# More score buffers, a third buffer for turned exponentials and two more PSUM banks in the last dilated attention pair

## Chip, cores and metric

The kernel runs on one core of a Trainium2 chip. The metric is device microseconds of one execution. The engines are TensorE (PE in the profile, its weight loads PEld), VectorE (DVE), ScalarE (ACT), GpSimd (POOL) and SyncE (SP), which only issues transfers. SBUF holds the tiles, PSUM the results of matmuls.

## What is computed

One step of a decoder layer, for a prompt of 1024 positions and eight single tokens ("samples") that read a cache. A combined projection of `x` (1024 channels) feeds eight dilated softmax heads of 64 channels and four gated DeltaNet heads of 128; their outputs, side by side, go through `w_out`, a LayerNorm, and a two-level mixture of 32 experts.

```python
p = x @ w_in
# dilated head, three branches (window, dilation) = (128,1), (512,4), (2048,16):
s = q @ k.T * Dh**-0.5 + bias;  pr = exp(s - max(s));  o = (pr @ v) / sum(pr)
oa = merge of the three branches, weighted by their softmax denominators
# DeltaNet heads give ob
h  = layer_norm(alpha * x + concat(oa, ob) @ w_out)
x' = layer_norm(alpha * h + hier_moe(h))
```

In the kernel the three branches are one softmax over all earlier positions: the merge is folded into the bias, which is a huge number where no branch reads a key.

## The kernel before

The work runs in this order: the DeltaNet heads with their projections; four pairs of dilated heads (0 to 3); the product with `w_out` and the LayerNorm in tiles of 128 positions (`mixed` and `finish`, lines 1136 and 1173), with the samples' attention in between; routing; the experts. Instructions are written in Python order, and a scheduler then sets the order on each engine; each engine works strictly in that order. A tile pool with n buffers lets the scheduler run a writer ahead of the readers of the n-1 tiles before.

**A pair** (`attention`, line 833) is eight row blocks `i` of 128 positions, two heads `j` each. For one (i, j), with w = 128 (i+1) columns: scores in pieces of at most 512 columns, two matmuls each (L857, L858), into PSUM tiles `s` of the pool `pss` (two banks); DVE adds the bias, writes them to the score buffer `sc` and takes the row minimum `mx` (L859); ACT takes the exponential in place (L864); PE turns `sc` in 128x128 blocks into PSUM tiles `pps` (L873, two banks); ACT (L875) or DVE (L877) copies them into `pT`; PE multiplies `pT` with the values into `o` (L882). After four row blocks the sums are inverted (L884, L885), turned (`rps`, L888), and the half's result `moa` is formed by ACT (L890) and DVE (L891) and stored (L892). `sc` uses the two buffers of the slot `ktl`, `pT` the two of `vh`.

While pairs 0 to 2 run, the projections of the next pair fill PE's waits (`next(fill, None)`). Pair 3 has no next pair. What stands beside it instead is: the loads of `w_out` on ACT's queue (L1059), the split of its rows into a rounded part on ACT (L1061) and the rest on DVE (L1062, the first of eight on POOL); the samples' products with cached keys on POOL (L911), summed on DVE (L912); and what the scheduler can bring forward of tile 0 of the product with `w_out`. For tile t this is two halves of 512 columns, 24 matmuls each (L1142), into `op`, in the pool `mm` of two PSUM banks that the projections used; their operands are `mh` (slot `qk`, buffer t%2; shown as `qkm`) and `ml` (slot `zt`, buffer (t+1)%2; shown as `ztm`), made from `mt` by ACT (L1167) and DVE (L1168). In the program's names `wst` and `wr` are loaded rows of `w_out`, `wo` their split, `kc` cached keys, `qb` the samples' queries, `g` and `b` the LayerNorm's factors (slot `U`, buffers 0 and 1, loaded on POOL's queue at L1120 and L1121).

```python
minima.setdefault(pr, []).append(ii)
...
if k not in WOP:
    after(los[-k - 1], minima[p_][n])
after(his[-k - 1], exps[p_][max(n - 1, 0)])
```

These lines (from the end of the driver) tie each subtraction and rounding of `w_out` behind a certain row minimum or exponential of the pair, by the table `WOD`; the cached keys' sums are tied in the same way.

## Time and profile before

| what | value |
|---|---|
| runs | 1508.02 us median of 3 (1506.76 to 1508.31) |
| profiled execution | 1508.93 us, its span 1507.2 us |
| busy share of the span | PE 94%, PEld 77%, DVE 72%, ACT 58%, POOL 21% |
| last dilated pair | 668.9 to 733.0 us |
| tiles 0 and 1 of the product with `w_out` | matmuls end 750.3 us |
| half clock in the pair | 678.7 to 709.5 us |

The span runs from the first to the last instruction. In a timeline row the first number is the start in us of the span, the second the length of the row (several instructions of one kind in succession make one row, xcount), and brackets give the idle time of the engine ahead of it with what ended it. A matmul's length includes its way through the array, so two in succession overlap; the distance of two starts is what one costs. PEclk is TensorE's granted clock, 1.00 being 2.4 GHz and 0.50 being 1.2 GHz. One matmul of L882 stands in the trace as up to two records, so the counts of `o` in the timeline are larger than in the program.

### The profile page before, as it was taken

How to read it: one execution, taken by the hardware profiler on the slowest of the kernel's cores; microseconds unless marked ns; L12 is line 12 of the kernel's file. 1: busy time of each engine (PE TensorE's matmuls, PEld its weight loads, DVE VectorE, ACT ScalarE, POOL GpSimd, SP SyncE). 2: the span in 40 equal slices, each digit the busy share in tenths (PEclk: the TensorE clock that was granted, in tenths of full speed). 3: DMA queues.
4: the chain of work that ended last, by engine and by line, in shares of the span. 5: the costliest groups of instructions: out<-in, count | busy, mean ns of one | idle time of the engine just before them, and what ended most of it. 6: DMA issues, size and time to landing. Idle time of an engine off the chain costs nothing. (4 is left out here: it accounts for less than half of the span.)

```text
span 1507.2 us, 22545 instructions
## 1 busy us (share of the span) xinstructions
PE 1410.2 (94%) x7916; PEld 1165.7 (77%) x7917; DVE 1084.3 (72%) x2080; ACT 878.8 (58%) x1747; POOL 319.5 (21%) x322
## 2 busy tenths in 40 slices
PE   6989999998999999999999969999999999999990
PEld 5879888887987878775777758888888888888870
DVE  3676776756444536356545669999999999999986
ACT  4323534333243434345221149999999999999984
POOL 1030403224032240112301121111111222111113
PEclk9999999999999999995999969999999999999995
DMA  5321101102332344054972569999999999999966
GB/s 197 115 77 36 59 28 42 36 10 76 92 115 95 108 138 120 32 158 143 265 251 88 209 236 352 356 368 375 353 360 348 356 372 362 365 360 368 345 212 230
DMA packets 115262, 309.36 MB, mean 205 GB/s; under 512 B 13635, under 2 KB 43255, under 8 KB 115136
## 3 DMA queue, kind: packets, MB, share of 16 engines
q1 hardware_dynamic: 89848, 261.74, 47.1%
q0 software_dynamic: 14640, 33.51, 8.9%
q10 hardware_dynamic: 10656, 12.62, 2.7%
q8 instruction: 64, 1.05, 0.3%
q14 instruction: 54, 0.44, 0.1%
HBM read 284.04 MB, written 45.24 MB: 218 GB/s over the span
## 5 line engine op out<-in xcount | busy, mean ns | idle before, releaser
L1362 DVE TENSOR_TENSOR wl<-p,wh 128x512 fp32r<-128x512 f32 x436 | 270.3, 686 | 1.7 <-ACT wh L1361 1.7
L1361 ACT CAST wh<-p 128x512 fp32r<-128x512 f32 x436 | 254.1, 633 | 19.3 <-PE h L1398 9.0
L278 PE MATMUL pp<-xh,w 128*128 128x344 f32 x672 | 231.8, 345 | 15.3 <-ACT xh L315 11.8
L280 PE MATMUL pp<-xh,w 128*128 128x344 f32 x672 | 223.1, 332 | 1.3 <-DVE w L253 1.3
L279 PE MATMUL pp<-xl,w 128*128 128x344 f32 x672 | 222.9, 332 | 0.6 <-DVE xl L316 0.6
L1396 PE MATMUL h<-wh,eh 128*128 128x512 f32 x512 | 207.1, 404 | 0.0
L1397 PE MATMUL h<-wl,eh 128*128 128x512 f32 x512 | 205.9, 402 | 0.4 <-DVE wl L1362 0.4
L1398 PE MATMUL h<-wh,el 128*128 128x512 f32 x512 | 201.2, 393 | 0.0
L278 PEld LDWEIGHTS pp<-xh,w 128*128 128x128 f32 x672 | 130.2, 194 | 26.9 <-ACT xh L315 11.5
L280 PEld LDWEIGHTS pp<-xh,w 128*128 128x128 f32 x672 | 129.9, 193 | 4.2 <-issue 1.9
L279 PEld LDWEIGHTS pp<-xl,w 128*128 128x128 f32 x672 | 130.2, 194 | 1.9 <-DVE xl L316 1.0
L1397 PEld LDWEIGHTS h<-wl,eh 128*128 128x128 f32 x512 | 96.8, 189 | 25.4 <-DVE wl L1362 7.9
L1362 DVE TENSOR_TENSOR wl_d<-p,wh_d 128x512 fp32r<-128x512 f32 x188 | 115.6, 687 | 0.0
L1368 POOL MEMSET xg<- 128x1024 f32 x32 | 30.5, 953 | 398.8 <-PE xp L1381 397.3
L1396 PEld LDWEIGHTS h<-wh,eh 128*128 128x128 f32 x512 | 96.9, 189 | 18.8 <-ACT eh L1383 0.2
L1361 ACT CAST wh_d<-p 128x512 fp32r<-128x512 f32 x188 | 109.4, 621 | 3.2
L1398 PEld LDWEIGHTS h<-wh,el 128*128 128x128 f32 x512 | 96.6, 189 | 18.8 <-DVE el L1384 0.2
L1437 PE MATMUL py<-wh_d,al 128*128 128x512 f32 x248 | 96.9, 391 | 0.0
L1435 PE MATMUL py<-wh_d,ah 128*128 128x512 f32 x248 | 96.6, 389 | 0.0
L1436 PE MATMUL py<-wl_d,ah 128*128 128x512 f32 x248 | 96.5, 389 | 0.0
L864 ACT ACTIVATE sc<-sc,mx 128x128 f32<-128x128 f32 (+7 forms) x64 | 49.7, 776 | 78.1 <-DVE mx L859 71.4
L1142 PE MATMUL op<-wo,qkm 128*128 128x512 f32 x256 | 84.8, 406 | 0.0
(457 smaller groups left out, 2764.5 us busy)
## 6 DMA issues: line engine op xcount, KB each, us to landing
p<-in_w_up SPq DMA_DIRECT2D x58, 1024.0 KB
p<-in_w_gate SPq DMA_DIRECT2D x51, 1024.0 KB
p<-in_w_down SPq DMA_DIRECT2D x47, 1024.0 KB
rw<-in_w_cols SPq DMA_DIRECT2D x28, 512.0 KB
p_vh<-in_w_down SPq DMA_DIRECT2D x12, 512.0 KB
p_ktl<-in_w_gate SPq DMA_DIRECT2D x10, 512.0 KB
p_ktl<-in_w_down SPq DMA_DIRECT2D x10, 512.0 KB
skew_d<-bias_d SPq DMA_DIRECT2D x1, 4608.0 KB
```

The source lines that it names most:

```text
L278: nc.tensor.matmul(ps, wh[:, k, :], xh[:, k, s], start=(k == 0), stop=False)
L279: nc.tensor.matmul(ps, wh[:, k, :], xl[:, k, s], start=False, stop=False)
L280: last[c0, g] = nc.tensor.matmul(ps, wl[:, k, :], xh[:, k, s], start=False, stop=(k == KD - 1))
L1142: mixes[t] = nc.tensor.matmul(pss[b], m[:, k, :], wo[k][:, w, cs[b]], start=(k + i == 0), stop=(k + i == KD + 1))
L1361: nc.scalar.copy(out=wh, in_=src)
L1362: nc.vector.tensor_tensor(out=wl, in0=src, in1=wh.bitcast(F32), op=OP.subtract)
L1396: nc.tensor.matmul(ps, eh[:, k, :], wh, start=(k == 0), stop=False)
L1397: nc.tensor.matmul(ps, eh[:, k, :], wl, start=False, stop=False)
L1398: nc.tensor.matmul(ps, el[:, k, :], wh, start=False, stop=(k == KD - 1))
L1435: nc.tensor.matmul(py[b], ah[:, k, :], wh, start=(k == 0), stop=False)
L1436: nc.tensor.matmul(py[b], ah[:, k, :], wl, start=False, stop=False)
L1437: nc.tensor.matmul(py[b], al[:, k, :], wh, start=False, stop=(k == 3))
```

## The change

Only pair 3 is touched (`pr == 3`). With u = 2i + j:

- **Scores:** odd row blocks put `sc` into buffer 0 of slot `U` (head 0) or of slot `qk` (head 1) instead of `ktl`: four buffers in turn instead of two.
- **Turned exponentials:** every third `pT` goes to buffer 1 of slot `zt`: three in turn instead of two.
- **PSUM:** for row blocks 0 to 5, the pieces with even u + n_ go to a bank of the pool `mm`, so half of the scores use the projections' two banks.

The three borrowed buffers have users behind the pair: `U` 0 is the LayerNorm's `g` (L1120), `qk` 0 is tile 0's `mh`, `zt` 1 is tile 0's `ml`. The two banks are those of tile 0's `op`. In the changed file, the lines behind 853 are shifted by up to 4: L857 to L861, L859 to L863, L864 to L868, L873 to L877, L882 to L886, L888 to L892, L1142 to L1146, L1168 to L1172.

```diff
--- before.py
+++ after.py
@@ -848,11 +848,15 @@
                 pTs = []
                 for j in range(2):
                     pt = slice(64 * j, 64 * j + 64)
-                    sc = T4("ktl", f"sc{pr}_{i}_{j}")
+                    u = 2 * i + j
+                    sc = T4("ktl", f"sc{pr}_{i}_{j}") if pr < 3 or u % 4 < 2 else T4_at(("U", "qk")[j], 0, f"sc{pr}_{i}_{j}")
                     mx = sm2.tile([P, 2], F32, tag="mx", name=f"mx{pr}_{i}_{j}", bufs=4)
                     cuts = (0, w) if w <= 512 else (0, 384 if w == 640 else 512, w)
                     for n_, (c, e) in enumerate(zip(cuts, cuts[1:])):
-                        sps = pss.tile([P, 512], F32, tag="s", name=f"s{pr}_{i}_{j}_{c}")
+                        if pr < 3 or i > 5 or (u + n_) % 2:
+                            sps = pss.tile([P, 512], F32, tag="s", name=f"s{pr}_{i}_{j}_{c}")
+                        else:
+                            sps = mm.tile([P, 512], F32, tag="mm", name=f"s{pr}_{i}_{j}_{c}")
                         qi = slice(i * P, (i + 1) * P)
                         nc.tensor.matmul(sps[:, :e - c], qs[j][:, qi], ks[j][:, c:e], start=True, stop=False)
                         nc.tensor.matmul(sps[:, :e - c], qs[j][pt, qi], kl[pt, c:e], start=False, stop=True)
@@ -864,7 +868,7 @@
                     ex = nc.scalar.activation(out=sc[:, :w], in_=sc[:, :w], func=AF.Exp, scale=-1.0, bias=m, accum_out=lsum[:, i, j:j + 1])
                     exps.setdefault(pr, []).append(ex)
                     next(fill, None)
-                    pT = tiles(T4("vh", f"pT{pr}_{i}_{j}"))
+                    pT = tiles(T4("vh", f"pT{pr}_{i}_{j}") if pr < 3 or u % 3 < 2 else T4_at("zt", 1, f"pT{pr}_{i}_{j}"))
                     pTs.append(pT)
                     for c in range(0, i + 1, 4):
                         e = min(i + 1, c + 4)
```

The order of the instructions shifts with it. In the rows below, `s_2_0_0` is the score piece of row block 2, head 0, first column 0; `pps`, `sc` and `pT` are numbered by block and head; `o_0` and `o_1` are the pair's two halves; the last number is the buffer's own.

PE, near the opening of pair 3, before:

```order
L873 MATMUL pps_0_0_0_6157<-cm,sc_0_0_6149 128x128
L873 MATMUL pps_0_1_0_6168<-cm,sc_0_1_6160 128x128
L882 MATMUL o_0_6148<-pT_0_0_6156,vv_6049 64x128
L882 MATMUL o_0_6148<-pT_0_1_6167,vv_6049 64x128
L857 MATMUL s_2_0_0_6203<-ksa_6119,qs_6118 128x384
L858 MATMUL s_2_0_0_6203<-kl_6121,qs_6118 128x384
L857 MATMUL s_2_1_0_6216<-ksb_6120,qs_6118 128x384
L858 MATMUL s_2_1_0_6216<-kl_6121,qs_6118 128x384
L873 MATMUL pps_1_0_0_6181<-cm,sc_1_0_6173 128x128 x2
L873 MATMUL pps_1_1_0_6193<-cm,sc_1_1_6185 128x128 x2
L882 MATMUL o_0_6148<-pT_1_0_6180,vv_6049 64x128
L857 MATMUL s_3_0_0_6235<-ksa_6119,qs_6118 128x512
```

and in the changed kernel, from the scores of block 2 on:

```order
L861 MATMUL s_2_0_0_6203<-ksa_6119,qs_6118 128x384
L862 MATMUL s_2_0_0_6203<-kl_6121,qs_6118 128x384
L861 MATMUL s_2_1_0_6216<-ksb_6120,qs_6118 128x384
L877 MATMUL pps_0_0_0_6157<-cm,sc_0_0_6149 128x128
L862 MATMUL s_2_1_0_6216<-kl_6121,qs_6118 128x384
L886 MATMUL o_0_6148<-pT_0_0_6156,vv_6049 64x128
L861 MATMUL s_3_0_0_6235<-ksa_6119,qs_6118 128x512
L862 MATMUL s_3_0_0_6235<-kl_6121,qs_6118 128x512
L861 MATMUL s_3_1_0_6249<-ksb_6120,qs_6118 128x512
L862 MATMUL s_3_1_0_6249<-kl_6121,qs_6118 128x512
L877 MATMUL pps_0_1_0_6168<-cm,sc_0_1_6160 128x128
L861 MATMUL s_4_0_0_6282<-ksa_6119,qs_6118 128x384
```

The scores of blocks 2, 3 and the beginning of 4 now stand ahead of the turning of block 1; before, the turning of blocks 0 and 1 stood between them.

PE, the end of pair 3 and what stands behind it, before (`op_0_6582` and `op_1_6583` are the halves of tile 0):

```order
L1142 MATMUL op_0_6582<-wo_6105,qkm_6572 128x512
L873 MATMUL pps_7_1_0_6484<-cm,sc_7_1_6472 128x128 x4
L873 MATMUL pps_7_1_4_6490<-cm,sc_7_1_6472 128x128 x4
L1142 MATMUL op_0_6582<-wo_6105,qkm_6572 128x512
L1142 MATMUL op_0_6582<-wo_6105,ztm_6573 128x512
L1142 MATMUL op_0_6582<-wo_6110,qkm_6572 128x512 x2
L888 MATMUL rps_1_6514<-cm,rlb_6146 128x128 x4
L1142 MATMUL op_0_6582<-wo_6110,ztm_6573 128x512
L1142 MATMUL op_0_6582<-wo_6115,qkm_6572 128x512
L882 MATMUL o_1_6279<-pT_7_1_6483,vv_6049 64x128
```

and in the changed kernel, from the pair's last `o` on (`scps` are the samples' scores):

```order
L886 MATMUL o_1_6279<-pT_7_1_6483,vv_6049 64x128
L892 MATMUL rps_1_6514<-cm,rlb_6146 128x128 x4
L923 MATMUL scps<-cm,sc_388 64x128
L924 MATMUL scps<-cm,sc_389 64x97
L1146 MATMUL op_0_6582<-wo_6082,qkm_6572 128x512 x2
L1146 MATMUL op_1_6583<-wo_6082,qkm_6572 128x512 x2
L1146 MATMUL op_0_6582<-wo_6082,ztm_6573 128x512
L1146 MATMUL op_0_6582<-wo_6086,qkm_6572 128x512 x2
```

Before, 22 of the 24 matmuls of tile 0's first half stood between the last blocks of the pair; now all 48 of the tile stand behind the pair, and the first that needs `ztm` is the fifth.

DVE at the same place, before (`ztm_6573` is tile 0's, `ztm_6673` tile 1's; the other 896 columns of tile 0 stand six rows further up):

```order
L1168 TENSOR_TENSOR ztm_6573<-mt_6571,qkm_6572 128x128
L877 COPY pT_7_0_6459<-pps_7_0_0_6460 128x512
L859 ISA sc_7_1_6472,mx_7_1_6473<-s_7_1_512_6478,tb_6142,mx_7_1_6473 128x512
L859 ISA mx_7_1_6473 128x1
L884 RECIPROCAL lsum_6145<-lsum_6145 128x8
L885 COPY rlb_6146<-lsum_6145 128x512
L877 COPY pT_7_1_6483<-pps_7_1_4_6490 128x512
L891 TENSOR_TENSOR moa_6147<-moa_6147,o_1_6279 128x512
L1176 SCALAR_TENSOR_TENSOR h_6580<-h_6580,op_0_6582 128x512
L1168 TENSOR_TENSOR ztm_6673<-mt_6671,qkm_6672 128x1024
```

and in the changed kernel:

```order
L888 RECIPROCAL lsum_6145<-lsum_6145 128x8
L889 COPY rlb_6146<-lsum_6145 128x512
L881 COPY pT_7_1_6483<-pps_7_1_4_6490 128x512
L1172 TENSOR_TENSOR ztm_6673<-mt_6671,qkm_6672 128x1024
L895 TENSOR_TENSOR moa_6147<-moa_6147,o_1_6279 128x512
L1172 TENSOR_TENSOR ztm_6573<-mt_6571,qkm_6572 128x896
L1172 TENSOR_TENSOR ztm_6573<-mt_6571,qkm_6572 128x128
L927 ISA avs,mxs<-scps,dbias 64x225
L927 ISA mxs 64x1
```

Tile 0's `ztm` moved from ahead of the last turned exponentials to behind the pair's last `moa`, and tile 1's from behind `moa` to ahead of it.

On ACT, tile 0's roundings (L1167) moved from ahead of block 7's exponentials to behind the last copy of `pT_7_1`, and tile 1's stands between block 7's two exponentials in both. Near the opening, the exponential of block 0, head 0, now stands ahead of the sixth load of `w_out` (L1059) on ACT's queue, and that of block 1, head 0, ahead of the seventh. On POOL the load of `g` moved from ahead of the pair to behind the samples' first loads of cached values.

## Rows read from the trace of the kernel before

**Rows 1.** The profile's page, part 1: busy us, share of the span, instructions.
```profile
PE 1410.2 (94%) x7916; PEld 1165.7 (77%) x7917; DVE 1084.3 (72%) x2080; ACT 878.8 (58%) x1747; POOL 319.5 (21%) x322
```

**Rows 2.** Windows of the last pair and tile 0: us, busy time per engine, PEclk, DMA.
```profile
668.90:678.70 9.80, 8.27 (x41) 5.00 (x40) 4.73 (x15) 2.90 (x11) 2.27 (x4) 1.00 0.95 317
678.70:709.50 30.80, 28.25 (x105) 17.24 (x105) 20.09 (x37) 15.55 (x28) 8.94 (x3) 0.50 0.40 145
709.50:733.00 23.50, 23.50 (x172) 16.75 (x169) 14.28 (x31) 11.26 (x20) 9.20 (x14) 1.00 0.74 199
733.00:750.30 17.30, 17.30 (x76) 13.96 (x76) 9.52 (x12) 1.05 (x1) 2.87 (x5) 1.00 1.05 287
```

**Rows 3.** Timeline of PE, opening of the pair: start, us, instruction, idle before.
```profile
674.00 0.71 PE L873 MATMUL pps<-cm,sc 128*128 128x128 f32 x2 [0.34 <-ACT sc L864]
...
678.05 1.02 PE L873 MATMUL pps<-cm,sc 128*128 128x128 f32 x4 [1.07 <-ACT sc L864]
...
679.62 0.80 PE L857 MATMUL s<-ksa,qs 128*128 128x512 f32 x1
680.34 0.79 PE L858 MATMUL s<-kl,qs 64*128 64x512 f32 x1
```

**Rows 4.** Timeline of ACT, same stretch: an exponential behind its queue's transfer.
```profile
677.39 0.51 ACT L864 ACTIVATE sc<-sc,mx 128x256 f32<-128x256 f32 x1 [2.38 <-DMA out_k_win<-kk]
```

**Rows 5.** Timeline of DVE: subtractions for w_out, two beside POOL's work, one alone.
```profile
684.97 2.68 DVE L1062 TENSOR_TENSOR wo<-wst,wo 128x1024 fp32r<-128x1024 f32 x1
...
688.19 2.77 DVE L1062 TENSOR_TENSOR wo<-wst,wo 128x1024 fp32r<-128x1024 f32 x1
...
695.47 1.22 DVE L1062 TENSOR_TENSOR wo<-wr,wo 128x1024 fp32r<-128x1024 f32 x1
```

**Rows 6.** Timeline of POOL, same stretch.
```profile
684.23 5.64 POOL L911 TENSOR_TENSOR kc<-kc,qb 128x1024 f32<-128x1024 f32 x2 [7.15 <-DMA qb<-qkv_d]
```

**Rows 7.** Timeline of PE, end of the pair and of the matmuls behind it.
```profile
719.70 0.49 PE L857 MATMUL s<-ksb,qs 128*128 128x512 f32 x1
720.12 0.50 PE L858 MATMUL s<-kl,qs 64*128 64x512 f32 x1
...
728.27 1.03 PE L873 MATMUL pps<-cm,sc 128*128 128x128 f32 x8
729.06 0.48 PE L1142 MATMUL op<-wo,qkm 128*128 128x512 f32 x1
...
731.14 1.96 PE L882 MATMUL o<-pT,vv 128*64 128x128 f32 x30
733.03 0.50 PE L1142 MATMUL op<-wo,qkm 128*128 128x512 f32 x1
...
750.29 0.60 PE L1188 MATMUL ht<-cm,h 128*128 128x128 f32 x4
```

**Rows 8.** Groups of PE by line and shape, 668.9 to 733.1 us.
```profile
L1142 PE MATMUL op<-wo,qkm 128*128 128x512 f32 x16 | 5.6, 413 | 0.0
...
L1142 PE MATMUL op<-wo,ztm 128*128 128x512 f32 x7 | 2.9, 421 | 0.0
```

**Rows 9.** Timeline of ACT, end of the pair.
```profile
720.76 1.15 ACT L864 ACTIVATE sc<-sc,mx 128x1024 f32<-128x1024 f32 x1 [1.01 <-DVE mx L859]
...
725.20 1.05 ACT L1167 CAST qkm<-mt 128x1024 fp32r<-128x1024 f32 x1
726.18 1.15 ACT L864 ACTIVATE sc<-sc,mx 128x1024 f32<-128x1024 f32 x1
...
730.78 0.59 ACT L890 COPY moa<-rps 128x512 f32<-128x512 f32 x1 [1.24 <-PE rps L888]
```

**Rows 10.** Timeline of DVE, end of the pair and first LayerNorm.
```profile
718.40 1.09 DVE L1168 TENSOR_TENSOR ztm<-mt,qkm 128x896 fp32r<-128x896 f32 x1
...
733.21 0.69 DVE L891 TENSOR_TENSOR moa<-moa,o 128x512 f32<-128x512 f32 x1 [3.18 <-PE o L882]
...
742.00 1.29 DVE L1008 SCALAR_TENSOR_TENSOR h<-h,mv,g 128x1024 f32<-128x1024 f32 x1
```

## The prediction

> **What bounds the kernel now.** I read the page first: PE is busy 94% of the span [rows 1], so a change off PE's path pays only where PE waits or runs slowly. The windows of the last pair show such a place [rows 2]: its three stretches last 9.8, 30.8 and 23.5 us, and in the second the granted clock is 0.50 (1.2 GHz) against 1.00 around it, although PE is busy 28.25 of the 30.8 us. Pair 3 is where no projections fill the waits. Behind it, from 733.00 to 750.30, PE is busy without a gap with tiles 0 and 1 of the product with `w_out`, and its matmuls go on in the same way; a pair that ends earlier therefore hands its gain on to the end of the program, us for us. So I ask one thing: when does PE finish the last `o` (L882) and the 96 matmuls (L1142) of tiles 0 and 1? Before, that is 733.03 and 750.29 [rows 7].
>
> The timelines show why PE loses time. At the opening PE waits 0.34 and 1.07 us for exponentials [rows 3], while ACT stands 2.38 us behind a transfer of its own queue [rows 4]; from about then on the clock is half. There a 512-column score matmul costs 0.72 us (679.62 to 680.34 [rows 3]), at full clock 0.42 (719.70 to 720.12 [rows 7]). Next DVE is the late engine: two subtractions for `w_out` take 2.68 and 2.77 us beside POOL's 5.64 us of products [rows 5, 6], a later one 1.22 alone, and scores and copies queue behind them. At the end the chain is one of latency: the two exponentials of block 7 start 5.4 us apart, at 720.76 and 726.18 [rows 9], and the turning (728.27) and the last `o` (731.14) follow [rows 7].
>
> **The change, part by part.** All is counted against the profiled execution, 1508.93 us; it lies 0.9 above the median of 1508.02.
>
> *No work is added.* The edits change buffers only, so every count stays. Choosing the slots costs nothing on the chip.
>
> *Opening.* With four score buffers and four banks the scores of blocks 2, 3 and part of 4 stand ahead of the turning of block 1. PE then has a dozen score matmuls of up to 0.42 us at hand, some 5 us, while ACT is late, and the exponentials of two blocks no longer stand behind ACT's loads. PE is busy 8.27 of 9.80 us there [rows 2], so 1.5 us of gaps are the least to be won if all close; ACT's wait of 2.38 is the most. I take 2.0.
>
> *Clock.* The clock fell just after those gaps and came back once PE had work in succession. If the opening closes, I expect it to fall only where DVE is late, at 685 instead of 679, and to come back some 4 us earlier, as scores wait ready: 10 us less of the 30.8. At full clock a score matmul spends 0.30 us less out of 0.72, or 0.42 per us; part of the stretch is waiting, which the clock does not change, so I take 0.35 per us, or 3.5 us. Bounds: nothing, if the stretch keeps its length, and 30.8 x 0.35 = 10.8, if there is none.
>
> *Tail.* Before, block 7's first exponential ends about 722.0 (720.76 + 1.15, and its sum's reading) and the last `o` ends at 733.03, 11.0 us later. Now the last score piece of block 7 stands among the `o` of block 6, ahead of the turning of block 7, and does not hold up the second exponential. The chain is then ACT's rounding for tile 1, which still stands between them, 1.05, the exponential with its reading 1.3 [rows 9], eight turnings 0.79 (728.27 to 729.06), a copy 0.6 to 0.7 (ACT's row of that shape is 0.59 [rows 9]), 30 records of `o` 1.89 (731.14 to 733.03) [rows 7], with some 0.3 between them: 6.0 us instead of 11.0. It wins 5.0, at most; nothing, if the copies on DVE or ACT come late.
>
> *The cover that is gone.* Before, 22 of tile 0's matmuls (of 23 records in this window [rows 8], the last starts at 733.03) filled exactly that chain. Now all 96 stand behind the pair. One costs (750.29 - 733.03) / 74 = 0.233 us [rows 7], so 5.1 us move to where nothing hides them. That is the price of the tail's gain, and the two nearly cancel.
>
> *A new wait.* Tile 0's `ml` now lies in the buffer of block 7's first `pT`, which only the last `o` frees; on DVE it stands behind `moa`, and that waits for the turned sums and for ACT. From the end E of the last `o`: four turnings for the sums 0.4, ACT's copy 0.59 [rows 9], `moa` 0.69, the 896 columns of `ml` 1.09 [rows 10], and 0.3 between them: E + 3.1. PE meanwhile has those turnings, two for the samples (0.2) and four matmuls with `mh` (0.9): E + 1.6. It waits 1.5 us with the other 92 matmuls queued behind (nothing, if `o` were freed early, 3 if DVE is still behind with tile 1's). All the samples' and LayerNorm's work behind shifts with it. The load of `g` on POOL moves behind the first loads of cached values; it is used first at 742.00 [rows 10], 9 us behind the pair, and I cost it at nothing. If POOL is late, that LayerNorm is, while PE still has tile 1 ahead.
>
> *Sum.* E = 733.0 - 5.0 - 2.0 - 3.5 = 722.5. The matmuls of both tiles end at E + 1.6 + 1.5 + 92 x 0.233 = E + 24.5 = 747.0, which is 3.3 to 3.4 us earlier than 750.3. So the change breaks even at E = 725.8. From the median: 1508.0 - 3.4 = **1504.6 us**. A measurement of this kernel can tell some 0.2%, 3.0 us, from no change, so the forecast stands just beyond that edge.
>
> **The lock between DVE and POOL.** The rows give the loss as 2.68 - 1.22 and 2.77 - 1.22, about 1.5 us per subtraction, and I assume the same again [rows 5, 6]. The Trainium skill ("SBUF — State Buffer", section "SBUF: two separate sides") says that an operation of VectorE with two SBUF inputs and one of GpSimd take a shared pair of ports as an exclusive lock, and that the later one stands still until the other ends. By that rule the loss would depend on where in POOL's operation the subtraction starts; one that starts together with a POOL operation of 2.8 us would lose all of it, and the two together 2.6 us more than I assume, which would put the sum at -0.8. The second row agrees with the rule: POOL's pair ends at 689.87, and 1.22 later is 691.09, against 690.96 measured.
>
> **Rivals.**
> 1. *The clock falls as before.* Against a shorter stretch: PE was busy 28.25 of 30.8 us and still held at half, and DVE's late stretch remains. Then the 3.5 us are missing: E = 726.0, and the result is within 0.3 us of before, about 1508. Two subtractions that each start together with a POOL operation of 2.8 us (5.64 / 2 [rows 6]) and lose all of it, 1.3 more each, would come to much the same, -0.8, and share this chance. The Trainium skill ("TensorE: Matmul & The Clock Gate", section "A second HAM failure mode: psum-queue depth-cycling") tells of a kernel whose TensorE paused briefly between groups of matmuls that cycle through PSUM banks, and whose clock swung between its two levels for that. By that rule four banks in turn would not hold the clock up; no run here has shown it yet.
> 2. *DVE paces the pair, and the cover is missed (slower).* The place is 685 to 694 on DVE: reductions of blocks 3 and 4 now crowd in ahead of the copies that PE's turning waits for, while the subtractions cost 2.7 each. Scores that are ready early do not help then. Without the gains of opening and clock, E = 728.0 and the result +2.2, some 1510; if the copies are late at the end too, the tail wins nothing, E = 733.0, and it is +7.2, some 1515. It decides from E = 725.8 on. For it: DVE's busy time lies there; against it: over the three windows DVE is busy 4.73 + 20.09 + 14.28 = 39.1 of 64.1 us [rows 2], so it has room on the whole.
> 3. *No half clock at all.* With PE fed throughout, E = 733.0 - 5.0 - 2.0 - 10.8 = 715.2 and the result -10.6, some 1497; with a third of the stretch left, -7, some 1501. For it: four buffers and banks double what PE can do ahead. Against it: DVE's subtractions stay.
>
> That the change does not do what it says is unlikely: the order shows the scores ahead and the borrowed slots have no later reader in the pair than their own.
>
> **Chances.** Forecast (1502.5 to 1506.5) 0.42; rival 1, 0.25; rival 2, 0.16; rival 3, 0.17. Faster by over 0.2% takes 0.30 of the forecast's share and rival 3: 0.47. Slower by over 3.0 us needs E above 728.8, the worse part of rival 2 and something for what I have not seen: 0.12. Within 0.2%: 0.41. For the range I leave out the far half of rival 3 and the worse half of rival 2: 1499.5 to 1511.0. The likeliest case's own range is 1502.5 to 1506.5.
>
> **What would show it.** Right, if the changed profile has the last `o` ending near 722.5, with a stretch at half clock of some 20 us that begins near 685, PE without gaps of over 0.3 us ahead of it, block 7's exponentials some 2.4 us apart, and a wait of about 1.5 us ahead of the first matmul with `ztm`. Wrong, if the half clock begins at 679 again (rival 1), if DVE's waits for PE vanish and PE's waits for `pT` and `mx` grow (rival 2), if the last `o` ends later than 725.8, or if the time gained at 750 is lost again behind it, in the LayerNorm of tile 0 or the samples' attention.

## The result, and the profile after

The changed kernel took 1521.01 us (median of 4 runs, 1520.01 to 1521.90) against 1508.16 of the kernel before beside it (4 runs): a ratio of 1.0081, 95% interval 1.0064 to 1.0097. The median is 12.9 us **slower**; the prediction was 1504.6 with a range of 1499.5 to 1511.0. Over all comparisons the kernel before ran between 1501.5 and 1515.6 us, so differences of a few us count below only as medians with their interval.

The two profiled executions differ by 11.1 us in their spans (1518.3 and 1507.2). I split that at places that both have, counted from the pair's first matmul on PE (668.86 before, 671.95 after):

| stretch | before | after | difference |
|---|---|---|---|
| start of the program to the pair | 668.86 | 671.95 | +3.09 |
| pair, to the end of the last `o` | 64.24 | 57.09 | -7.15 |
| from there to the turning of tile 0's LayerNorm (`ht`) | 17.19 | 34.00 | +16.81 |
| from there to the end of PE's wait for the experts' first tokens (`xg`) | 138.23 | 136.48 | -1.75 |
| rest | 618.68 | 618.78 | +0.10 |

The first row is no effect of the change: the order of the work there is the same, and the start of the pair scattered from 666.3 to 673.9 us over the eighteen kernels profiled for this study. The pair gained 7.15 us, two thirds of what I had forecast. The third row took that back twice over. Without the first row the two executions differ by 8.0 us; the interval of the runs is 9.7 to 14.6, so a part of the loss is not seen in this pair of profiles.

The windows of the changed kernel (us, busy time per engine, PEclk, DMA share, GB/s; the pair in three stretches, the matmuls of tiles 0 and 1, and what follows) answer to [rows 2]:

```profile
671.95:684.90 12.95, 11.38 (x55) 6.76 (x52) 7.33 (x23) 4.59 (x14) 1.70 (x3) 1.00 0.92 297
684.90:712.00 27.10, 25.50 (x101) 15.97 (x101) 19.10 (x33) 13.70 (x26) 8.96 (x3) 0.50 0.34 125
712.00:729.04 17.04, 16.33 (x135) 11.42 (x135) 10.99 (x24) 10.65 (x18) 5.86 (x9) 0.99 0.69 190
729.04:753.40 24.36, 23.10 (x103) 18.41 (x102) 6.76 (x12) 1.36 (x4) 5.77 (x9) 1.00 1.04 263
753.40:764.20 10.80, 1.37 (x6) 1.17 (x6) 5.10 (x6) 2.10 (x3) 1.85 (x2) 0.65 0.34 108
```

The half clock is still there, 27.1 us of it instead of 30.8. The last row is new: PE is busy 1.37 us of 10.80, and the granted clock falls once more. The timeline of PE around the end of the pair and of the matmuls behind it answers to [rows 7]:

```profile
727.08 1.96 PE L886 MATMUL o<-pT,vv 128*64 128x128 f32 x30 [0.29 <-ACT pT L879]
...
729.61 1.17 PE L1146 MATMUL op<-wo,qkm 128*128 128x512 f32 x4
732.04 0.50 PE L1146 MATMUL op<-wo,ztm 128*128 128x512 f32 x1 [1.26 <-DVE ztm L1172]
...
753.21 0.40 PE L1146 MATMUL op<-wo,ztm 128*128 128x512 f32 x1
763.04 1.12 PE L1192 MATMUL ht<-cm,h 128*128 128x128 f32 x4 [9.43 <-DVE h L1013]
```

Up to 753 all is much as forecast: the wait for `ml` is 1.26 us, and the matmuls of the two tiles end some 24.5 us behind the last `o`. Then PE stands 9.43 us for tile 0's LayerNorm on DVE; before, the matmuls ran straight into `ht` at 750.29 [rows 7]. DVE of the changed kernel shows why:

```profile
730.29 0.69 DVE L895 TENSOR_TENSOR moa<-moa,o 128x512 f32<-128x512 f32 x1
730.90 1.29 DVE L1172 TENSOR_TENSOR ztm<-mt,qkm 128x896 fp32r<-128x896 f32 x2
...
758.28 1.23 DVE L1172 TENSOR_TENSOR ztm<-mt,qkm 128x1024 fp32r<-128x1024 f32 x1 [14.42 <-ACT qkm L1171]
759.43 0.20 DVE L1007 BATCH_NORM_AGGREGATE mv<-bn 128x2 f32<-128x12 f32 x1
759.66 1.28 DVE L1012 SCALAR_TENSOR_TENSOR h<-h,mv,g 128x1024 f32<-128x1024 f32 x1
761.70 1.29 DVE L1013 SCALAR_TENSOR_TENSOR h<-h,mv,b 128x1024 f32<-128x1024 f32 x1 [0.75 <-POOL mv L1009]
```

The row at 758.28 is the subtraction for tile **2**. It stands ahead of tile 0's LayerNorm in DVE's order, and DVE idles 14.42 us for it, with 3.6 us of LayerNorm behind it (759.43 to 762.99) that PE needs. The same order stood in the kernel before and did no harm, as these rows of its DVE show (the row that follows is in [rows 10]):

```profile
740.63 1.21 DVE L1168 TENSOR_TENSOR ztm<-mt,qkm 128x1024 fp32r<-128x1024 f32 x1
741.76 0.20 DVE L1003 BATCH_NORM_AGGREGATE mv<-bn 128x2 f32<-128x12 f32 x1
```

What the subtraction waits for is a load. ACT and its queue (ACTq) in the changed kernel:

```profile
720.73 1.15 ACT L868 ACTIVATE sc<-sc,mx 128x1024 f32<-128x1024 f32 x1 [0.95 <-DVE mx L863]
...
722.70 1.05 ACT L1171 CAST qkm<-mt 128x1024 fp32r<-128x1024 f32 x1 [0.73 <-PE s L861]
723.99 1.15 ACT L868 ACTIVATE sc<-sc,mx 128x1024 f32<-128x1024 f32 x1 [0.24 <-DVE mx L863]
...
730.15 0.30 ACT L1171 CAST qkm<-mt 128x128 fp32r<-128x128 f32 x1
730.34 2.25 ACTq L1170 DMA_DIRECT2D mt<-mixd  x2
...
757.21 1.05 ACT L1171 CAST qkm<-mt 128x1024 fp32r<-128x1024 f32 x1 [24.00 <-DMA mt<-mixd]
```

and in the kernel before:

```profile
721.71 0.37 ACTq L1166 DMA_DIRECT2D mt<-mixd  x1
...
739.07 1.05 ACT L1167 CAST qkm<-mt 128x1024 fp32r<-128x1024 f32 x1 [7.70 <-PE op L1142]
```

Tile 2's operands load into the buffer of tile 0's, which is free once tile 0 is rounded (730.15 on ACT) and subtracted (730.90 on DVE, to 732.19). Both wait for the pair now, because they write into borrowed buffers. So tile 2's load, the second of the two in the row at 730.34, goes out at 732.2 instead of 721.71 (counted from the pair's start that is 7.4 us later). By the landing events in the traces it lands 24.9 us behind its issue, where before it took 13.2. Two things now stand ahead of it. One is the load of tile 3, which has come before it in the order of ACT's queue (the tiles' `mt` are 6571, 6671, 6767 and 6985):

```
L1171 CAST qkm_6572<-mt_6571 128x128
L1170 DMA mt_6985<-mixd 128x8x128
L1170 DMA mt_6767<-mixd 128x8x128
...
L1171 CAST qkm_6768<-mt_6767 128x1024
```

The other is the next stage's weights; the issues of SP's queue in the changed kernel, and then before:

```profile
717.65 3.97 SPq L967 DMA_DIRECT2D p_ktl<-in_w_gate  x2
723.12 0.46 SPq L967 DMA_DIRECT2D p_z<-in_w_down  x1
723.97 5.48 SPq L967 DMA_DIRECT2D p_vh<-in_w_down  x2
```

```profile
724.75 0.35 SPq L963 DMA_DIRECT2D p_ktl<-in_w_gate  x1
725.37 0.33 SPq L963 DMA_DIRECT2D p_z<-in_w_down  x1
729.37 0.33 SPq L963 DMA_DIRECT2D p_ktl<-in_w_gate  x1
732.93 0.33 SPq L963 DMA_DIRECT2D p_vh<-in_w_down  x1
...
734.36 0.44 SPq L963 DMA_DIRECT2D p_vh<-in_w_down  x1
```

Five pieces of 512 KB stand in slots that the pair used and that it leaves earlier now. Before, tile 2's load was ahead of all five; now it is behind all five, with the DMA engines busy throughout (share 1.04).

### The profile page after: what moved, and what is told of

The parts are those of the page before. It is cut to its first block, busy times and chain, and to the rows that moved or that the text cites. A ratio compares the mean times of both kernels' runs of the same rounds, so it can differ in the third digit from the quotient of the medians.

```text
span 1518.3 us, 22531 instructions
## 1 busy us (share of the span) xinstructions
PE 1410.3 (93%) x7916; PEld 1166.3 (77%) x7917; DVE 1084.5 (71%) x2080; ACT 880.0 (58%) x1747; POOL 322.4 (21%) x322
## 5 line engine op out<-in xcount | busy, mean ns | idle before, releaser
L278 PE MATMUL pp<-xh,w 128*128 128x344 f32 x672 | 232.1, 345 | 16.4 <-ACT xh L315 13.1
L280 PE MATMUL pp<-xh,w 128*128 128x344 f32 x672 | 223.8, 333 | 1.3 <-DVE w L253 1.3
L279 PE MATMUL pp<-xl,w 128*128 128x344 f32 x672 | 223.1, 332 | 0.6 <-DVE xl L316 0.6
L278 PEld LDWEIGHTS pp<-xh,w 128*128 128x128 f32 x672 | 130.5, 194 | 28.2 <-ACT xh L315 12.7
L868 ACT ACTIVATE sc<-sc,mx 128x128 f32<-128x128 f32 (+7 forms) x64 | 49.8, 778 | 73.5 <-DVE mx L863 73.2
L1146 PE MATMUL op<-wo,qkm 128*128 128x512 f32 x256 | 85.0, 407 | 0.0
```

The lines of the kernel that those rows point to most:

```text
L278: nc.tensor.matmul(ps, wh[:, k, :], xh[:, k, s], start=(k == 0), stop=False)
L279: nc.tensor.matmul(ps, wh[:, k, :], xl[:, k, s], start=False, stop=False)
L280: last[c0, g] = nc.tensor.matmul(ps, wl[:, k, :], xh[:, k, s], start=False, stop=(k == KD - 1))
L1146: mixes[t] = nc.tensor.matmul(pss[b], m[:, k, :], wo[k][:, w, cs[b]], start=(k + i == 0), stop=(k + i == KD + 1))
```

## Experiments

Edits are against the changed kernel unless another is named. `ht` is the turning of tile 0's LayerNorm on PE. Pair lengths and half clock are those of one profiled execution each (half clock: 2 x length of the pair x (1 - its mean PEclk); PEclk has two digits, which leaves some 0.6 us open). These executions are not typical ones: the profiled one was the fastest of its kernel for the change, the banks only, the third turned buffer only, the weights held back and "the same, LayerNorm first", and the slowest for LayerNorm first and tile 2's load first. The ratio is that of all runs of the kernel to the runs of the kernel before that were taken beside them (medians from 1508.2 to 1510.3 us); it is not the quotient of medians, and the two differ by up to 0.14%.

| kernel | median us (runs) | ratio to before, interval | pair, us | half clock in it | `ht` behind the pair's start | end of the experts' wait behind it |
|---|---|---|---|---|---|---|
| before | 1508.16 (4) | | 64.2 | 30.8 | 81.4 | 219.7 |
| the change | 1521.01 (4) | 1.0081 (1.0064 to 1.0097) | 57.1 | 27.4 | 91.1 | 227.6 |
| banks only | 1508.48 (10) | 1.0001 (0.9985 to 1.0016) | 58.1 | 7.0 | 75.3 | 214.1 |
| four score buffers only | 1517.64 (6) | 1.0067 (1.0038 to 1.0096) | 58.2 | 26.8 | 90.0 | 228.4 |
| third turned buffer only | 1515.93 (10) | 1.0046 (1.0032 to 1.0060) | 59.5 | 30.9 | 87.7 | 223.7 |
| nothing borrowed in the last blocks | 1516.76 (10) | 1.0041 (1.0024 to 1.0058) | 71.4 | 37.1 | 91.1 | 227.5 |
| the same, rounding tied | 1511.31 (10) | 1.0027 (1.0006 to 1.0048) | 56.1 | 16.8 | 82.8 | 218.1 |
| LayerNorm first | 1512.89 (10) | 1.0017 (0.9996 to 1.0038) | 57.5 | 27.6 | 81.9 | 223.8 |
| weights held back | 1510.77 (10) | 1.0018 (0.9995 to 1.0041) | 53.7 | 17.2 | 78.1 | 217.3 |
| both ties | 1513.07 (12) | 1.0024 (1.0008 to 1.0041) | 57.4 | 27.6 | 81.8 | 226.3 |
| banks, third buffer early | 1510.52 (10) | 1.0005 (0.9984 to 1.0026) | 64.6 | 31.0 | 83.6 | 219.9 |
| banks, 40 transposes | 1505.16 (12) | 0.9981 (0.9966 to 0.9997) | 58.9 | 3.5 | 76.1 | 214.7 |
| **banks, 80 transposes** | **1502.91** (6) | **0.9958** (0.9946 to 0.9971) | 58.2 | 0.0 | 75.2 | 212.8 |
| before, 80 transposes | 1505.86 (12) | 0.9991 (0.9975 to 1.0006) | 61.9 | 7.4 | 79.3 | 217.5 |
| the change, 80 transposes | 1510.82 (12) | 1.0017 (0.9999 to 1.0034) | 57.9 | 6.9 | 84.1 | 223.1 |
| weights held, 80 transposes | 1507.74 (12) | 0.9978 (0.9963 to 0.9993) | 57.9 | 6.9 | 80.4 | 217.2 |
| tile 2's load first | 1514.43 (12) | 1.0032 (1.0014 to 1.0049) | 60.0 | 33.6 | 87.9 | 226.9 |
| the same, LayerNorm first | 1512.77 (12) | 1.0028 (1.0008 to 1.0048) | 53.8 | 17.2 | 78.2 | 217.0 |

### One part of the change at a time

The banks alone: both borrowing lines undone.

```diff
-                    sc = T4("ktl", f"sc{pr}_{i}_{j}") if pr < 3 or u % 4 < 2 else T4_at(("U", "qk")[j], 0, f"sc{pr}_{i}_{j}")
+                    sc = T4("ktl", f"sc{pr}_{i}_{j}")
...
-                    pT = tiles(T4("vh", f"pT{pr}_{i}_{j}") if pr < 3 or u % 3 < 2 else T4_at("zt", 1, f"pT{pr}_{i}_{j}"))
+                    pT = tiles(T4("vh", f"pT{pr}_{i}_{j}"))
```

> Only the PSUM part of the change: half of the scores of blocks 0 to 5 through the projections' banks, two score buffers and two turned buffers as before. Theory (late release: buffers whose last user is block 7 hold up tile 0's operands, hence the load of tile 2's operand, hence, on DVE, tile 0's LayerNorm, for which PE waits 9.4 us): no such buffer is borrowed here, the load for tile 2 is issued near 722 us as before, PE does not wait ahead of L1192, and the time is within 3 us of before. Rival (DMA crowding: the score slots come free earlier, so weight pieces start earlier and slow the load for tile 2): also no change. If this alone is slower by over 3 us, both fall and it is the banks.

The four score buffers alone (the piece always in `pss`, `pT` in `vh`), and the third turned buffer alone:

> Only the four score buffers; two turned buffers, two banks. Theory: the buffer of tile 0's rounded operand is held by block 7, head 1, so tile 0 stands behind the pair, the load for tile 2 is issued some 10 us late, PE waits 5 to 10 us ahead of the first L1192, and the time is 6 to 14 us above before. Rival (DMA crowding): weight pieces start near 718 us, same sign, 6 to 14 us. No change (within 3 us) would leave the third turned buffer as the cause.

> Only the third turned buffer. Theory: the rest of tile 0's operand waits for the last o matmul, the load for tile 2 is issued near 732 us, though ahead of that for tile 3 on its queue, so it lands some 10 us earlier than in the changed kernel: PE waits 0 to 6 us ahead of L1192, the time is 1 to 8 us above before. Rival (DMA crowding by the score slots): scores keep their slots, weights start as before, so within 3 us of before.

The banks alone cost nothing, 1.0001. Each kind of borrowing alone costs most of the loss, 1.0067 and 1.0046. In both, the rounding of tile 2 waits for the load; ACT of the kernel with four score buffers, then PE of the two:

```profile
752.10 1.04 ACT L1171 CAST qkm<-mt 128x1024 fp32r<-128x1024 f32 x1 [21.81 <-DMA mt<-mixd]
```

```profile
757.93 1.12 PE L1192 MATMUL ht<-cm,h 128*128 128x128 f32 x4 [7.23 <-DVE h L1013]
```

```profile
756.74 1.12 PE L1192 MATMUL ht<-cm,h 128*128 128x128 f32 x4 [5.56 <-DVE h L1013]
```

With the banks alone `ht` follows the matmuls with no wait:

```profile
745.07 0.60 PE L1192 MATMUL ht<-cm,h 128*128 128x128 f32 x4
```

So the loss belongs to the borrowed buffers, and either is enough: one holds up tile 0's rounding, the other its subtraction, and the load needs both. One sign missed: with the third turned buffer alone the load landed 21.0 us behind its issue, 3.9 sooner than in the change and not 10.

### Borrowing nothing in the last blocks

```diff
-... if pr < 3 or u % 4 < 2 else T4_at(("U", "qk")[j], 0, ...
+... if pr < 3 or i > 5 or u % 4 < 2 else T4_at(("U", "qk")[j], 0, ...
-... if pr < 3 or u % 3 < 2 else T4_at("zt", 1, ...
+... if pr < 3 or u > 11 or u % 3 < 2 else T4_at("zt", 1, ...
```

> The whole change, but blocks 6 and 7 take no borrowed buffer (scores in the old two, turned exponentials of the last four in the old two), so the borrowed ones are free for tile 0 before the pair ends. Theory: the load for tile 2 is issued before the last o, no wait of over 2 us ahead of L1192, and the gain of the opening shows: 1 to 6 us below before. Rival (DMA crowding): weight pieces start as in the kernel before, so no slower than before either; the two differ in when the load for tile 2 lands after its issue: under 10 us by the theory, some 20 us by the rival.

This did not go as expected: 1.0041. The loads of tiles 1 and 2 went out at 720.39 and 722.56, but now **tile 1's** rounding waited for its own, on ACT, ahead of the last copy of `pT`:

```profile
738.49 1.05 ACT L1171 CAST qkm<-mt 128x1024 fp32r<-128x1024 f32 x1 [10.33 <-DMA mt<-mixd]
739.44 0.58 ACT L879 COPY pT<-pps 128x512 f32<-128x512 f32 x1
```

```profile
740.08 3.67 PE L886 MATMUL o<-pT,vv 128*64 128x128 f32 x30 [9.66 <-ACT pT L879]
```

It is the same mechanism one tile earlier: a load that lands 18.1 us behind its issue (3.8 in the changed kernel), and an engine that stands for it ahead of work that PE needs. Tile 2's load landed 24.8 us behind its issue, which is the rival's sign and not the theory's. The next kernel ties that rounding behind the pair's last copy and is otherwise the same:

```diff
+        after(his["m", 1], copies["pT"])
```

> The variant in which blocks 6 and 7 borrow nothing, with one tie: ACT rounds tile 1's operand behind the pair's last copy of turned exponentials. Theory (in that variant ACT stood in its own order before a load of 18 us, 9.7 us of PE's waiting): the wait ahead of the last o goes; tile 1's matmuls come 11 us later than the last o, when the load is there; 1 to 5 us below before. Rival (the time is set by when the loads land, wherever the wait stands): a wait of 3 to 9 us shows ahead of tile 1's or tile 2's matmuls, 1 to 7 us above before.

The wait of 9.66 us is gone, the time is 1511.31, and the rival's wait shows: 4.33 us ahead of tile 1's matmuls, for DVE's sum of tile 0, which stands behind tile 1's late subtraction.

```profile
743.14 1.19 PE L1146 MATMUL op<-wo,qkm 128*128 128x512 f32 x2 [4.33 <-DVE h L1180]
```

### The late load itself: who waits, and why it is late

LayerNorm first: DVE's subtraction for tile 2 is tied behind tile 0's LayerNorm. Nothing else of DVE's order changes.

```diff
+        after(marks["ml", 2], marks["n", "1_0"])
```

> The changed kernel with one tie: on DVE, tile 2's subtraction (L1172) stands behind tile 0's LayerNorm instead of ahead of it. Theory (the load for tile 2 comes late and, in DVE's order, its subtraction holds up tile 0's LayerNorm): the wait of 9.4 us ahead of the first L1192 goes, and some 4 us of it come back as a wait for tile 2's rounded operand, which still lands some 85 us behind the start of the pair; 3 to 6 us faster than the changed kernel, so 6 to 10 us above before. Rival (the LayerNorm is late for another reason, its factor g or POOL): the wait stays, 10 to 13 us above before.

Weights held back: the pieces that come in two loads are issued a tile later in the program and wait for tile 2's load.

```diff
-PIECE_AT = {3: (8, 4, 2, 3), 4: (6,)}
+PIECE_AT = {2: (5, 7), 3: (8, 4, 2, 3), 4: (6,)}
...
+            if len(ts) == 2:
+                tc.add_manual_dep(ld.ins, loads["mt", 2].ins.name, ...
```

> The changed kernel, but the five weight pieces in the slots of scores, turned exponentials and pair results start only when the load for tile 2 has landed. Crowding theory (the late load is slow since the weight pieces, which now start 7 us earlier, share the DMA engines with it): it lands within 15 us of its issue instead of 25, the wait ahead of L1192 falls to 0 to 3 us, 2 to 6 us above before. If only its late issue counts, or the loads on POOL's queue crowd it: it still takes 20 us or more, 9 to 13 us above before.

Both bring 8 to 10 us back, the LayerNorm more than its theory's 3 to 6, and neither can be told from the kernel before any more (both intervals include 1). With the LayerNorm first, PE has no wait at `ht`, and one of 3.06 us later instead, for the sum of tile 1 (L1180), which still stands behind tile 2's subtraction on DVE:

```profile
753.57 0.60 PE L1192 MATMUL ht<-cm,h 128*128 128x128 f32 x4
757.23 1.19 PE L1146 MATMUL op<-wo,qkm 128*128 128x512 f32 x2 [3.06 <-DVE h L1180]
```

With the weights held back, ACT's rounding comes some 14 us behind the issue instead of 25; the load lands 13.9 us behind it, close to the 13.2 of before, and PE has no wait at `ht` although the load still goes out late:

```profile
721.32 2.24 ACTq L1173 DMA_DIRECT2D mt<-mixd  x2
737.15 1.05 ACT L1174 CAST qkm<-mt 128x1024 fp32r<-128x1024 f32 x1 [12.96 <-DMA mt<-mixd]
```

The Trainium skill ("DMA: Bandwidth & Descriptors", section "Issuing engines are not separate DMA queues") says that transfers started by different engines run on the same 16 DMA engines and interleave there. The trace agrees: ScalarE issued the load and SyncE the weights, and the one took 11 us less when the others were held.

Both ties together:

> The whole change, with the weights' pieces held back until tile 2's load has landed and DVE's subtraction for tile 2 behind the LayerNorm of tile 0. Theory (the loss lies in tile 2's late load and in DVE standing for it): with either tie alone 8 to 10 us of 11 to 13 came back, 1510.8 and 1512.9; both wins work on the same wait, so together they give little more than the better one: 1508 to 1511, no wait of PE over 1 us ahead of tile 0's turned LayerNorm, and the pair still 54 to 58 us. Rival (a second cost of the change lies elsewhere, in the lost cover of 5 us or behind the LayerNorms): 1511 or more, with both waits gone. Rival 2 (the two ties remove different losses and the pair's gain of 7 us comes through): 1501 to 1505.

1513.07, no better than either alone and in the range of the first rival. No wait is left at `ht`, but another of 4.32 us for ACT appears farther on (`junk`, L1210).

Tile 2's load first: only two loads on ACT's queue change places, no matmul and nothing on DVE; and then with the LayerNorm first as well.

```diff
+        after(loads["mt", 3], loads["mt", 2])
```

> The whole change, with tile 2's load ahead of tile 3's on ACT's queue (in the change tile 3's stands first; with the 80 transposes and with the third turned buffer alone tile 2's does). Theory (much of what the transposes won in the whole change, 1521.0 to 1510.8, was this order of the two loads, and not the clock): the load lands in 17 to 20 us instead of 25, PE's wait for tile 0's LayerNorm is 2 to 6 us instead of 9.4, and the time 1512 to 1517. Rival (the two loads share the engines anyway, and the transposes' gain was the clock): 1518 to 1522 with a wait of 8 us or more. Rival 2 (the order alone gives all of it back): 1508 to 1511.

> As the kernel before in this list, with DVE's subtraction for tile 2 also behind tile 0's LayerNorm. Theory (the late load is all of the loss, and what is left of the change is the pair's gain of 7 us against 5 us of lost cover): 1506 to 1510, no wait of PE for the LayerNorm, and no other wait of over 1.5 us up to the samples. Rival (the change has a cost of its own beyond the late load): 1511 to 1515.

The order of these two loads alone brings 1.0081 down to 1.0032. The first theory holds: the load lands 18 to 19 us behind its issue, and the wait at `ht` is 3.41 us.

```profile
752.08 1.05 ACT L1171 CAST qkm<-mt 128x1024 fp32r<-128x1024 f32 x1 [17.97 <-DMA mt<-mixd]
```

```profile
757.92 0.66 PE L1192 MATMUL ht<-cm,h 128*128 128x128 f32 x4 [3.41 <-DVE h L1013]
```

So the load was late three times over: it went out later, behind tile 3's, and behind 2.5 MB of weights. The last two have an experiment each; the late issue has none of its own, but with the weights held back PE had no wait at `ht` in spite of it. The second kernel has no wait at `ht`, but its 1512.77 is in the range of the rival. Mended in any of these ways, the change is left at 1.0017 to 1.0032, never below before. The table shows why, as far as single executions can: with no wait at `ht` and the pair at half clock for 27.6 us, `ht` comes 81.9 or 81.8 us behind the pair's start, against 81.4 before. The pair's gain pays for the cover of tile 0 and no more. In the two profiled with 17.2 us of half clock it comes at 78.1 and 78.2, and these were the fastest runs of their kernels. What is left goes with the clock; that the clock decides it is argued here and not shown.

### Is it the clock?

The banks with a third score buffer in slot `U` for row blocks 0 to 4 only, where no tile of the product waits for it:

> The PSUM part and one more score buffer, in the slot of the LayerNorm's factor g, for blocks 0 to 4 only; tile 0's operands keep their buffers. Theory: no load is late, all 22 matmuls of tile 0 stay inside the pair, and the opening's gain shows: 1 to 5 us below before. Rival (the pair's length is set by when the clock falls, not by buffers): within 1.5 us of before on the median, with runs that scatter by 5 us with their clock.

No difference, 1.0005, as the rival has it; in this execution the pair ran at half clock for 31.0 us and was as long as before. The execution of the banks alone that was profiled had 7.0 us of it, and its pair took 58.1:

```profile
669.74:689.00 19.26, 15.08 (x83) 9.08 (x80) 12.05 (x25) 9.42 (x22) 6.20 (x6) 1.00 0.69 229
689.00:698.00 9.00, 8.10 (x35) 5.25 (x35) 7.41 (x14) 4.67 (x8) 5.02 (x2) 0.62 0.30 100
698.00:727.88 29.88, 27.35 (x199) 19.26 (x198) 20.19 (x44) 15.66 (x28) 9.23 (x14) 1.00 0.78 231
```

Yet its ten runs have the median of before: this execution is the fastest of them, with the highest mean clock (0.968 at 1503.35 us; the slowest has 0.956 at 1514.51). Nor do short waits alone tell when the clock falls: in its first 19.26 us PE was busy 15.08, and the clock stayed at 1.00. To hold the clock by hand, 4 or 8 transposes of the identity go ahead of each turning of row blocks 1 to 5 (into the tile that the turning overwrites; no result uses them), on top of the banks:

```diff
+                        if pr == 3 and 1 <= i <= 5 and c == 0:
+                            for q in range(8):
+                                nc.tensor.transpose(ps[:, q % 4, :], ident, ident)
```

> The banks alone, with four more transposes of the identity in front of each turning of row blocks 1 to 5 (80 or more in all at 0.1 us at full clock, some 4 us of work that no result uses, partly inside PE's waits). Theory that the half clock of the pair is what PE's short waits cause and that it costs some 5 to 8 us: with the waits filled the clock stays at 1.00 in the pair, the pair is 56 to 60 us in spite of the added work and the result -2 to -6 against before. Rival (the clock falls all the same or the time is DVE's and ACT's): the half clock stays, the pair is 62 us or more and the result is 0 to +6.

> As with four, but eight more transposes in front of each turning of row blocks 1 to 5, some 8 us of work that no result uses. Theory (clock): the clock stays at 1.00 more surely, but the work beyond the waits costs: 0 to 4 us later than with four. Rival (the pair is paced by DVE and ACT, and PE's added work is hidden): no difference to four, within 1 us. Rival 2 (the added work is on PE's path throughout): 4 us later or more.

Both are faster than before: 0.9981 and **0.9958** (0.9946 to 0.9971), 5.4 us less, although PE does 40 and 80 transposes more (four ahead of each turning are 40, not the 80 of the expectation). By its median the larger addition wins more, where I had expected it to cost more than four; the two intervals overlap. With 40, the order on every engine is that of the banks alone but for the transposes and five score matmuls of blocks 4 and 5. With 80, a few instructions on DVE, ACT and POOL change places too, so a part of the 5.4 us may be the order's. The windows of the pair with 80 transposes, in stretches as long as the first two of [rows 2]:

```profile
669.57:679.40 9.83, 9.81 (x53) 6.47 (x51) 5.54 (x17) 3.42 (x11) 2.27 (x4) 1.00 0.95 314
679.40:710.20 30.80, 29.03 (x218) 21.52 (x217) 25.57 (x48) 19.05 (x35) 9.29 (x3) 1.00 0.49 172
710.20:727.73 17.53, 17.53 (x130) 12.79 (x127) 8.32 (x19) 7.49 (x13) 9.22 (x14) 1.00 0.88 228
```

PE is busy 9.81 of the first 9.83 us (before 8.27 of 9.80), and the clock stays at 1.00 throughout; over its six runs the mean clock is 0.967 to 0.970, against 0.956 to 0.968 with the banks alone. That the first stretch is full does not decide it: with the weights held back and no transposes PE was busy 9.79 of the first 9.80 us, and the clock still fell 12.7 us into the pair. The same transposes in the kernel before, in the whole change, and in the change with the weights held back:

> The kernel before, with eight more transposes of the identity ahead of each turning of row blocks 1 to 5 of the last pair (80 in all, which no result uses). With the two banks the same addition gave 1502.9 against 1508.3. Theory A (the clock is all there is to it, the banks are worth nothing): 1501 to 1505 here too, granted clock of the mean over the span 0.967 or more in every execution. Theory B (without the banks the scores cannot run ahead, PE's added work lies on its path and the clock still falls for lack of scores): 1506 to 1511.

> The whole change with the same 80 transposes. Theory (two separate losses: the half clock, and the borrowed buffers' late load): the clock is kept, some 5 us come back, and the late load still costs its 9 to 13: 1512 to 1517, with a wait of PE of 5 us or more for tile 0's LayerNorm. Rival (the late load only hurts because the pair ran slowly): 1503 to 1508. Rival 2 (added work delays the pair and nothing is kept): 1519 or more.

> The whole change with the same 80 transposes and with the weights' pieces held back until tile 2's load has landed. Theory (with both losses gone, what is left of the change is the earlier end of the pair, 54 us, against 5 us of lost cover and the wait of 1.3 for ml): 1503 to 1507, level with the two banks and the transposes alone (1502.9) or 1 to 4 above. Rival (the whole change is worth its 7 us once the rest is mended): 1496 to 1500. Rival 2 (a loss not yet found): 1508 or more.

In the kernel before they give 0.9991, no difference that can be told, although the mean clock over a run rose from 0.956 to 0.965 up to 0.964 to 0.971. The clock is mostly kept (7.4 us of half clock in the profiled pair), but without the banks that pair takes 61.9 us, 3.7 more than with them. The median lies between my two theories: banks and transposes were worth 0.42% together and neither a measurable part alone. Here too the scheduler moved other instructions along with the transposes (on ACT the loads and roundings of tile 0, for one), so the three kernels do not isolate the clock.

With the whole change, 1510.82 lies between theory and rival. The wait at `ht` is 3.52 us, not the 5 I asked for, and the pair is no shorter than the change's own.

```profile
754.29 0.66 PE L1195 MATMUL ht<-cm,h 128*128 128x128 f32 x4 [3.52 <-DVE h L1016]
```

The transposes had moved tile 2's load ahead of tile 3's as well; that order alone gave 1514.43, so of the 10 us most is the load's and at most the rest the clock's. With the weights held as well the ratio is 0.9978, a little below before, and 1507.74 falls between theory and rival 2. By the quotients of the medians the first and the last of the three change places (0.9978 and 0.9991), so these two are not told apart. Neither goes beyond the banks with 80 transposes: nothing shows that the buffers add to those.

## Why the prediction was wrong

**The step that failed** stands at the end of "A new wait": "All the samples' and LayerNorm's work behind shifts with it. The load of `g` on POOL moves behind the first loads of cached values … I cost it at nothing." I followed the three borrowed buffers to their next users (`g`, `mh`, `ml`) and priced those, but not what those release. `mh` and `ml` of tile 0 free the buffer that tile 2 loads into; ACT's rounding and DVE's subtraction of tile 2 stand ahead of tile 0's LayerNorm. That chain cost PE 9.43 us. The load of `g` itself was indeed free (L1012 starts without a wait, also at 744.27 in the kernel with the LayerNorm first). Shown: each borrowing alone brings the wait, the banks alone do not, and mending the load or its place on DVE takes most of the loss away. My last sentence had named the place ("the LayerNorm of tile 0"), with no price and no share of the chances beyond 0.12.

By its own steps, in the profiled executions:

- **Opening (-2.0): not shown.** ACT's wait of 2.38 us behind its queue is gone, as forecast. But the idle time of PE before the half clock is 12.95 - 11.38 = 1.57 us, as before (1.53). The gaps moved from ACT's exponentials to DVE's minima, which is the mechanism of rival 2, at less than its price. PE of the changed kernel:

```profile
682.60 0.38 PE L861 MATMUL s<-ksb,qs 128*128 128x256 f32 x1 [0.68 <-DVE mx L863]
...
684.93 0.68 PE L861 MATMUL s<-ksb,qs 128*128 128x384 f32 x1 [0.90 <-DVE mx L863]
```

- **Clock (-3.5): right price, wrong length.** It fell at 685, as forecast, but by luck: this pair started 3.1 us later. Counted from the pair's start the clock fell 12.95 us in (before 9.8, forecast 16.1) and came back 40.05 us in (before 40.6, forecast 36.1), so 3.7 us of half clock went and not 10. The price holds as far as single executions show it: between the change and the change with weights held back, 10.2 us less of half clock go with a pair 3.4 us shorter, 0.33 per us against my 0.35; between the last two kernels of the table it is 16.4 and 6.2 us, 0.38.
- **Tail (-5.0): 4.0.** From the start of block 7's first exponential to the end of the last `o` it is 8.3 us (720.73 to 729.04) instead of 12.3; the two exponentials are 3.3 us apart, not 2.4, as tile 1's rounding between them waited 0.73 us for PE's last scores and DVE's minimum came 0.24 late.
- **Cover gone (+5.1) and `ml` (1.5): right.** From the end of the last `o` to the end of both tiles' matmuls I had 24.5 us; it was 34.00 - 9.43 = 24.6, with 1.26 for `ml`.
- **The sum.** Of the 7.15 us that the pair gained, 4.0 are the tail's and 1.3 what 3.7 us of half clock are worth at my price; no run here attributes the rest. The pair was to end 53.6 us after its start (722.5 - 668.9), and ended at 57.1. At that point the two tiles end at 81.7 instead of 81.4: the gain was already nothing, beyond my break-even. Then came 9.4 us of the wait, 1.75 of which was regained behind it, and 3.1 that this execution had lost ahead of the pair.

**The rivals.** Rival 1 (about 1508) gave the right neighbourhood for a kernel without the late load: the mended kernels and the banks alone lie within 0.32% of before. Its other half, a larger loss to the lock between DVE and POOL, did not come: the three subtractions beside POOL's work took 1.52, 2.91 and 2.51 us (before 2.68, 2.77 and 2.17). In both kernels each of them ends 1.1 us behind the POOL operation that it began beside, so the loss is about what is left of that operation. Two rows of the changed kernel:

```profile
689.01 3.33 POOL L915 TENSOR_TENSOR kc<-kc,qb 97x1024 f32<-97x1024 f32 x1
```

```profile
690.53 2.91 DVE L1066 TENSOR_TENSOR wo<-wst,wo 128x1024 fp32r<-128x1024 f32 x1
```

Of the clock I had said that four banks might not hold it up. The Trainium skill ("TensorE: Matmul & The Clock Gate", section "A second HAM failure mode: psum-queue depth-cycling") blames brief pauses between groups of matmuls for a swinging clock. The runs agree as far as they go: with four banks in turn and PE's pauses left as they were, one profiled pair had 7.0 us of half clock and another (with the third buffer early) 31.0, and the mean clocks of the ten runs with the banks alone, 0.956 to 0.968, lie about where those of the kernel before lie, 0.956 to 0.964; with the pauses filled, the profiled pairs had 3.5 and 0.0. That banks in turn matter beside the pauses, no run shows. Rival 2 was on the right side of zero for the wrong reason: DVE paced PE not inside the pair but 25 us behind it, by standing for a load. Rival 3's 1497 was not reached by any median; the best, without half clock, is 1502.9.

**What stays open:** why the half clock in the pair lasts 27 us in one execution and 17 or 7 in others of nearly the same program, whether the clock or the order brings the 5.4 us of the banks with 80 transposes, and why the start of the pair scatters by 7.6 us.

## What to carry to other kernels

When a change borrows a buffer, follow the chain beyond the buffer's next user: what does that user release, which load starts on it, which queue is it then behind, and what stands behind the load's consumer on its in-order engine. Price the cover that the borrowing takes away before the gain it brings; here the two cancelled to half a microsecond, in executions with about the half clock of before, even without the late load. And where PE shows half clock between short waits, put work into the waits as a test before restructuring: 80 useless transposes together with the two free banks were worth 5.4 us, more than any buffer.

## What the hardware showed that I had not expected

The same load of 512 KB landed about 25 us behind its issue in the crowd, 18 to 19 with its place in the queue exchanged for that of one other load, and some 14 with the weights held back (13.2 in the kernel before). A pair whose first 9.83 us PE filled to 9.81 kept a granted clock of 1.00 to its end; with 8.27 of 9.80 half clock followed for 30.8 us. That is no rule: the change with the weights held back filled 9.79 of its first 9.80 us, and half clock followed for 17.2. And the fastest of the eighteen kernels does 80 transposes more than before that no result uses.
